# The first norm's vector moved into the first eight units of weights, and the end weighed by VectorE alone

## The chip, the cores and the metric

The kernel runs on one core of a Trainium2 chip. The metric is the device time of one execution in microseconds (us); lower is better. A core has five engines that run beside each other, each through its own instructions in order: TensorE (PE, matrix products, with its weight loads, PEld), VectorE (DVE), ScalarE (ACT), GpSimd (POOL) and SyncE (SP), which here issues the loads. They wait for each other through semaphores.

## The reference

Two layers on x (256 rows of 1024 numbers). A layer is a half-step SwiGLU, a mixing sub-layer of attention and spatial gating, and a second half-step SwiGLU; each has an RMS norm ahead of it and another behind it:

```python
def rms_norm(x, g):
    return x * rsqrt(mean(x * x, axis=-1) + RMS_EPS) * g

def swiglu(x, w1, w2):
    g, u = split(x @ w1, 2, axis=-1)
    return (silu(g) * u) @ w2

for l in range(DEPTH):
    h = rms_norm(x, ffn1_pre_g[l])
    x = x + 0.5 * rms_norm(swiglu(h, ffn1_w1[l], ffn1_w2[l]), ffn1_post_g[l])
    ...                                     # the mixing sub-layer
    h = rms_norm(x, ffn2_pre_g[l])
    x = x + 0.5 * rms_norm(swiglu(h, ffn2_w1[l], ffn2_w2[l]), ffn2_post_g[l])
```

The change is in the first `rms_norm` of the first layer, the product that follows it, and the last `rms_norm`.

## The kernel before

**Numbers as a sum of two.** Each float32 operand of a product is split into a high part, rounded to the format that TensorE reads (a rounding copy on ScalarE), and a low part, the rest (a subtraction on VectorE). A product is three passes into the same PSUM bank: high by high, high by low, low by high (`passes`, L252).

**The stream of weights.** All weights come in units of 128 x 1024 numbers (512 KB) in the order of their use. `Stream.load` issues a unit's load on SyncE into one of four buffers (`raw`, L119). `Stream.upto(n)` splits the units up to number n - 1: ScalarE's copy (L138), VectorE's subtraction (L152), and then the load that may reuse the buffer, four units on. A product calls for its unit by itself if the program has not split it before. The order of the instructions on every engine is the order in which the program's lines run (a manual schedule): what stands later in the program stands later in each engine's queue.

**The start.** The 256 rows are two tiles, t = 0 and 1; a tile has two halves of 512 features, h = 0 and 1 (four blocks of 128 features each). The program loads x in halves, between the first units. TensorE warms up on the identity (`warm`, L972), and transposes x's halves (L217). `weigh` (L943) multiplies them by the norm's vector g0, and `high0` (L947) and `low0` (L950) split them. The first eight units, 0 to 7, are the first 512 columns of w1's gate half (units 0 to 3) and of its other half (units 4 to 7). They are multiplied by rows that are weighed but not yet divided by their root mean square; `finish` scales the result (L314, L315). Unit u needs the blocks 2 (u mod 4) and the next one of both tiles: 12 multiplications of 128x512. Units 0, 1, 4 and 5 use the half h = 0, the others h = 1. `some`, `part` and `units` only write out the order.

**The hand-over.** Meanwhile ScalarE sums the squares of x (L177), VectorE makes the two reciprocal roots (`rsqrt`, L185 to L200) and puts them on two diagonals (L232), and TensorE spreads them over all partitions (`spread`, L239), from which ScalarE copies `rb` (L241). VectorE multiplies each quarter (tile t, half h) by it (L1023), and the quarter is split into `xt` (L947 and L950 again). From unit 8 on, `feature_pair` (L272) multiplies by `xt`: its first four instructions need the quarters with h = 0, the fifth those with h = 1. Before, the program calls for units 5, 6 and 7 ahead of unit 4's products, for unit 8 after the two quarters of tile 0, and for unit 9 after those of tile 1.

**The end.** `project` without a next sub-layer (L467 to L511) adds the last product's norm to x. For tile 1, ScalarE sums squares (L177) and takes a root (L488), VectorE refines its reciprocal in two rounds (L500, L505), and the second half of the product is weighed by the norm's vector in two pieces: VectorE takes 128 columns (L502) and GpSimd 384 (L495), from a copy that ScalarE makes (L494), since GpSimd can't read PSUM here. Then VectorE adds both halves (L444) and they are stored.

Of the kernel before, what the change touches and what calls it, by code (L numbers as in the profile page):

```python
# [14 lines left out]
F32R = mybir.dt.float32r  # L15
# [5 lines left out]
P = 128  # L21
D = 1024
# [29 lines left out]
TURN = 1  # L52
TURN1 = 1

CUT = 128

WARM = (11, 8)

ATTEND = (27, 32, 38, 44, 50, 56)
GATING = (9, 10, 11, 12)  # L60
# [3 lines left out]
def trunk(ctx: ExitStack, tc: tile.TileContext, a: dict, out: bass.AP):  # L64
# [35 lines left out]
    class Stream:  # L100
        def __init__(self):
            self.src, self.where = [], []
            self.raw, self.split = {}, {}
            self.loaded = self.ready = 0
            self.free = RING
            self.rest = None
            self.slip = False

        def add(self, src, where="ring"):
            self.src.append(src)  # L110
            self.where.append(where)
            return len(self.src) - 1

        def load(self, n):

            while self.loaded < min(n, len(self.src)):
                u = self.loaded
                self.raw[u] = new(rawp, [P, 1024], "raw")
                nc.sync.dma_start(self.raw[u], self.src[u])  # L119
                self.loaded += 1  # L120

        def upto(self, n, spare=0):


            while self.ready < min(n, len(self.src)):
                u = self.ready
                if self.where[u] == "ring":
                    if self.free <= spare:
                        return
                    self.free -= 1  # L130
                self.load(u + 1)
                if self.where[u] == "ring":
                    h, lo = new(ring, [P, 1024], "wh", F32R), new(ring, [P, 1024], "wl", F32R)
                else:
# [3 lines left out]
                nc.scalar.copy(h, self.raw[u])  # L138
                self.split[u] = (h, lo)
                self.ready += 1  # L140
                self.low()
                self.rest = u
                if not self.slip:
                    self.low()

        def low(self):

            if self.rest is not None:
                u = self.rest
                self.rest = None  # L150
                h, lo = self.split[u]
                nc.vector.tensor_tensor(out=lo, in0=self.raw.pop(u), in1=f(h), op=ALU.subtract)  # L152
                self.load(u + 1 + RAW)

        def __getitem__(self, u):
# [16 lines left out]
    def halves():  # L172
        return [slice(h * 512, (h + 1) * 512) for h in range(2)]
# [229 lines left out]
    def project(units, lhs, k_post, gpost, gpre, nxt, xt, behind=None):  # L403
# [63 lines left out]
        if nxt is None:  # L467

            root = new(tiny, [P, 1], "rb")
            nc.scalar.activation(root, ones[:, 0:1], AF.Sqrt)  # L470
            head(0)
            c = new(t2, [P, 512], "t2")
            nc.scalar.copy(c, o[0][1])
            nc.gpsimd.tensor_tensor(out=og[0][:, 512:D], in0=c, in1=gpost[:, 512:D], op=ALU.mult)
            r, = rsqrt([(total(parts[0]), k_post)])
            for h, b in enumerate(halves()):
                add(0, h, r)
                nc.sync.dma_start(out[rows_of(0), b], xs[0][:, b])

            head(1)  # L480
            k = 0.25 ** k_post
            vb = new(tiny, [P, 1], "rv")
            nc.vector.tensor_scalar(out=vb, in0=parts[1][:, 0:1], scalar1=D * RMS_EPS, scalar2=k, op0=ALU.add,
                                    op1=ALU.mult)
# [3 lines left out]
            nc.scalar.activation(root, parts[1][:, 1:2], AF.Sqrt, bias=vb, scale=k)  # L488
            w = new(tiny, [P, 1], "rw")
            nc.vector.scalar_tensor_tensor(out=w, in0=parts[1][:, 1:2], scalar=-0.5 * k, in1=vw, op0=ALU.mult,  # L490
                                           op1=ALU.add)
            c0, c1, c2 = 512, 512 + CUT, D
            c = new(t2, [P, 512 - CUT], "t2")
            nc.scalar.copy(c, o[1][1][:, CUT:])  # L494
            nc.gpsimd.tensor_tensor(out=og[1][:, c1:c2], in0=c, in1=gpost[:, c1:c2], op=ALU.mult)  # L495
            r = new(tiny, [P, 1], "ry")
            nc.vector.reciprocal(r, root)
            for i in range(2):
                v = new(tiny, [P, 1], "rt")
                nc.vector.scalar_tensor_tensor(out=v, in0=r, scalar=w, in1=r, op0=ALU.mult, op1=ALU.mult)  # L500
# [4 lines left out]
                nc.vector.scalar_tensor_tensor(out=y, in0=v, scalar=1.5, in1=r, op0=ALU.add, op1=ALU.mult)  # L505
# [405 lines left out]
    for b in halves():  # L911
        nc.sync.dma_start(xs[0][:, b], a["x"][0:P, b])
    st.load(1)
    for b in halves():
        nc.sync.dma_start(xs[1][:, b], a["x"][P:2 * P, b])
# [22 lines left out]
    def quarter0(t, h):  # L938
        return slice(None), slice(h * 4, h * 4 + 4), rows_of(t)

    def weigh(t, h, ps):
        ks = slice(h * 4, h * 4 + 4)
        nc.vector.tensor_tensor(out=xg[t][:, ks, :], in0=ps, in1=g0[:, ks].unsqueeze(2).to_broadcast([P, 4, P]),  # L943
                                op=ALU.mult)

    def high0(x, t, h):
        nc.scalar.copy(x[0][quarter0(t, h)], xg[t][:, h * 4:h * 4 + 4, :])  # L947

    def low0(x, t, h):
        nc.vector.tensor_tensor(out=x[1][quarter0(t, h)], in0=xg[t][:, h * 4:h * 4 + 4, :],  # L950
                                in1=f(x[0][quarter0(t, h)]), op=ALU.subtract)

    one = []
    for t in range(NT):
        first.begin(t)
        one.append(first.steps(t, *xu)[3])

    def units(u, tiles=range(NT)):

        for t in tiles:  # L960
            for k in range(2):
                one[t](u // 4, u % 4 * 2 + k)

    def part(u, t, which):

        for k in range(2):
            one[t](u // 4, u % 4 * 2 + k, which)

    def warm(n):

# [2 lines left out]

    cold = bank()
    warm(WARM[0])
    ps = [transpose4(xs[0], h * 4) for h in range(2)]
    weigh(0, 0, ps[0])
    weigh(0, 1, ps[1])
    high0(xu, 0, 0)
    low0(xu, 0, 0)  # L980
    st.upto(1)
    high0(xu, 0, 1)
    low0(xu, 0, 1)
    warm(WARM[1])
    part(0, 0, (0, 2))
    ps = [transpose4(xs[1], h * 4) for h in range(2)]
    part(0, 0, (1,))
    weigh(1, 0, ps[0])
    st.upto(2)
    high0(xu, 1, 0)  # L990
    low0(xu, 1, 0)
    weigh(1, 1, ps[1])
    part(1, 0, (0, 2))
    part(0, 1, (0, 1))
    part(1, 0, (1,))
    st.upto(3)
    high0(xu, 1, 1)
    low0(xu, 1, 1)
    part(0, 1, (2,))
    part(2, 0, (0, 2))  # L1000
    part(1, 1, (0, 1, 2))
    st.upto(5)
    part(2, 0, (1,))
    part(2, 1, (0, 1, 2))
    sums = []
    for t in range(NT):
        parts = new(tiny2, [P, 2], "parts")
        for h, b in enumerate(halves()):
            square(parts, h, xs[t][:, b])
        sums.append(parts)  # L1010
    r01 = rsqrt([(total(parts), 5) for parts in sums])
    dg = diagonal(r01)
# [7 lines left out]
    for t in range(NT):  # L1020
        for h in range(2):
            ks = slice(h * 4, h * 4 + 4)
            nc.vector.tensor_tensor(out=xg[t][:, ks, :], in0=xg[t][:, ks, :], in1=bc4(rb[:, t, :]), op=ALU.mult)  # L1023
            high0(xt, t, h)
            low0(xt, t, h)
        st.upto(9 + t)
        units(5 + t)
    units(7)
    st.upto(8 + AHEAD)
    subs[0].prepare()  # L1030
# [79 lines left out]
```

## Time and profile before

| what | value |
|---|---|
| median of 3 runs | 1188.09 us (1187.77 to 1188.12) |
| the profiled execution | 1190.44 us, its span 1188.7 us |
| TensorE busy | 1173.2 us, 99% of the span |
| VectorE, ScalarE, GpSimd busy | 836.3, 678.4, 60.0 us |
| read from HBM | 218.65 MB, 185 GB/s over the span |
| TensorE's first multiplication by weights, and its run without gaps | from 7.86, from 10.81 us |
| last multiplication | starts at 1180.93 us |

The span goes from the first to the last instruction of the program; the profiled execution's time has 1.74 us around it. A row of a timeline has the start, the duration, the engine, the line, the operation, what it writes and reads (names without buffer numbers, shapes), and how many instructions are merged; in brackets stands the idle time of the engine before it and what ended it. A row of the groups has the line, engine, operation, shapes and count, then busy us and mean ns of one, then idle time. A row of the chain of waits has start, duration and what the end of the kernel was waiting for at that time.

### The profile page before, as it was taken

How to read it: one execution, taken by the hardware profiler on the slowest of the kernel's cores; microseconds unless marked ns; L12 is line 12 of the kernel's file. 1: busy time of each engine (PE TensorE's matmuls, PEld its weight loads, DVE VectorE, ACT ScalarE, POOL GpSimd, SP SyncE). 2: the span in 40 equal slices, each digit the busy share in tenths (PEclk: the TensorE clock that was granted, in tenths of full speed). 3: DMA queues.
4: the chain of work that ended last, by engine and by line, in shares of the span. 5: the costliest groups of instructions: out<-in, count | busy, mean ns of one | idle time of the engine just before them, and what ended most of it. 6: DMA issues, size and time to landing. Idle time of an engine off the chain costs nothing.

```text
span 1188.7 us, 18407 instructions
## 1 busy us (share of the span) xinstructions
PE 1173.2 (99%) x7031; PEld 1044.6 (88%) x7031; DVE 836.3 (70%) x1423; ACT 678.4 (57%) x1143; POOL 60.0 (5%) x40
## 2 busy tenths in 40 slices
PE   8999999998999999999999999999999999999997
PEld 7888888998999888888888888889999998888886
DVE  6768748778685976666586666578878668676753
ACT  5656644547676555664455665455577664665541
POOL 0000000001112100000000000000011040000000
PEclk9999999999999999999999999999999999999999
DMA  7577673554456636657725767645644653565660
GB/s 248 179 247 227 229 245 134 193 196 142 127 154 202 210 107 213 207 183 263 227 95 179 235 202 238 216 154 178 201 139 140 192 193 129 178 199 198 197 204 36
DMA packets 61288, 220.90 MB, mean 186 GB/s; under 512 B 7056, under 2 KB 7056, under 8 KB 61200
## 3 DMA queue, kind: packets, MB, share of 16 engines
q1 hardware_dynamic: 60912, 219.46, 56.8%
q8 instruction: 55, 0.90, 0.3%
q14 instruction: 33, 0.27, 0.1%
q10 hardware_dynamic: 288, 0.27, 0.1%
HBM read 218.65 MB, written 1.05 MB: 185 GB/s over the span
## 4 chain that ended last, share of the span: by engine, by line
PE 92%; DVE 3%; DMA 3%; ACT 1%; issue 1%; SPq 0%; DVEq 0%; ACTq 0%
PE mm L272 34%; PE mm L252 33%; PE mm L259 7%; PE mm L260 7%; PE mm L261 7%; DMA raw<-in_w_in 2%; PE mm L217 1%; PE mm L756 1%; DVE wl L152 1%; PE mm L720 1%; PE mm L719 1%; DMA raw<-in_ffn_w 1%; PE mm L769 0%; PE mm L768 0%; ACT wh L138 0%
## 5 line engine op out<-in xcount | busy, mean ns | idle before, releaser
L152 DVE TENSOR_TENSOR wl<-raw,wh 128x1024 fp32r<-128x1024 f32 x372 | 455.6, 1250 | 117.5 <-ACT wh L138 116.1
L138 ACT CAST wh<-raw 128x1024 fp32r<-128x1024 f32 x372 | 383.0, 1050 | 177.3 <-DMA raw<-in_ffn_w 70.4
L272 PE MATMUL mm<-xt,wh 128*128 128x512 f32 x1152 | 290.7, 393 | 0.7 <-DVE xt L950 0.7
L252 PE MATMUL mm<-wh,m 128*128 128x512 f32 x832 | 258.4, 390 | 0.0
L272 PEld LDWEIGHTS mm<-xt,wh 128*128 128x128 f32 x1152 | 207.3, 189 | 38.6 <-DVE xt L950 1.2
L252 PEld LDWEIGHTS mm<-wh,m 128*128 128x128 f32 x832 | 156.2, 188 | 32.1
L272 PEld LDWEIGHTS mm<-xt,wl 128*128 128x128 f32 x1152 | 157.1, 190 | 11.3
L252 PE MATMUL mm<-wl,m 128*128 128x512 f32 x416 | 161.9, 389 | 0.0
L272 PE MATMUL mm<-xt,wl 128*128 128x256 f32 x1152 | 160.6, 282 | 0.0
L259 PE MATMUL mm<-xt,wh 128*128 128x256 f32 x512 | 146.8, 287 | 0.0
L261 PE MATMUL mm<-xt,wl 128*128 128x256 f32 x512 | 145.3, 284 | 0.0
L260 PE MATMUL mm<-xt,wh 128*128 128x256 f32 x512 | 145.3, 284 | 0.0
L634 DVE TENSOR_TENSOR t<-mm,t 128x256 f32<-128x256 f32 x144 | 60.6, 421 | 97.0 <-ACT t L633 97.0
L260 PEld LDWEIGHTS mm<-xt,wh 128*128 128x128 f32 x512 | 98.8, 193 | 0.2
L259 PEld LDWEIGHTS mm<-xt,wh 128*128 128x128 f32 x512 | 98.8, 193 | 0.2
L261 PEld LDWEIGHTS mm<-xt,wl 128*128 128x128 f32 x512 | 98.6, 193 | 0.0
L252 PEld LDWEIGHTS mm<-wl,m 128*128 128x128 f32 x416 | 78.1, 188 | 16.0
L633 ACT COPY t<-mm 128x256 f32<-128x256 f32 x144 | 52.9, 368 | 46.6 <-PE mm L272 46.5
L259 PE MATMUL mm<-m,wh 128*128 128x256 f32 x256 | 72.5, 283 | 0.0
L260 PE MATMUL mm<-m,wh 128*128 128x256 f32 x256 | 72.4, 283 | 0.0
L261 PE MATMUL mm<-m,wl 128*128 128x256 f32 x256 | 72.4, 283 | 0.0
L636 ACT ACTIVATE t<-t 128x256 f32<-128x256 f32 x72 | 30.1, 418 | 73.8 <-DVE t L634 73.8
(156 smaller groups left out, 1324.3 us busy)
## 6 DMA issues: line engine op xcount, KB each, us to landing
raw<-in_ffn_w SPq DMA_DIRECT2D x264, 512.0 KB, 4.5
raw<-in_w_in SPq DMA_DIRECT2D x84, 512.0 KB, 4.3
raw<-in_w_sgu_branch SPq DMA_DIRECT2D x16, 512.0 KB, 3.7
raw<-in_w_attn_branch SPq DMA_DIRECT2D x16, 512.0 KB, 4.3
raw<-in_w_out SPq DMA_DIRECT2D x16, 512.0 KB, 4.6
gain<-in_ffn_post_g SPq DMA_DIRECT2D x4, 512.0 KB, 6.5
gain<-in_ffn_pre_g SPq DMA_DIRECT2D x3, 512.0 KB, 7.4
x<-in_x SPq DMA_DIRECT2D x4, 256.0 KB, 4.3
```

The lines of the kernel that those rows point to most:

```text
L138: nc.scalar.copy(h, self.raw[u])
L152: nc.vector.tensor_tensor(out=lo, in0=self.raw.pop(u), in1=f(h), op=ALU.subtract)
L217: nc.tensor.transpose(ps[:, k, :], src[:, (c0 + k) * P:(c0 + k + 1) * P], ident)
L252: nc.tensor.matmul(o, every[i][0], every[i][1], start=start and i == 0, stop=stop and i == 2)
L259: nc.tensor.matmul(o, wh[:, ks], ah[:, k, :], start=(k == 0), stop=False)
L260: nc.tensor.matmul(o, wh[:, ks], al[:, k, :], start=False, stop=False)
L261: nc.tensor.matmul(o, wl[:, ks], ah[:, k, :], start=False, stop=(k == KD - 1))
L272: nc.tensor.matmul(out_, w[:, k * P:(k + 1) * P], x, start=(i == 0), stop=(i == len(todo) - 1))
L633: nc.scalar.copy(y[:, half, :], o[half][:, S:2 * S])
L634: nc.vector.tensor_tensor(out=y[:, half, :], in0=o[half][:, 0:S], in1=y[:, half, :], op=ALU.add)
L636: nc.scalar.activation(y[:, 0, :], y[:, 0, :], AF.Silu)
L719: nc.tensor.matmul(s[r][:, i, :], q_, kth[:, g, 0:nk], start=True, stop=False)
```

## The change

Four things. The first transfers are ordered anew: x's half (0, 0), unit 0 in two halves, x's half (1, 0), unit 1, x's halves (0, 1) and (1, 1), units 2 and 3. The norm's vector g0 is taken out of the rows and put into units 0 to 7 while these are split: each half of a unit (one block of features) is rounded by an activation with a scale (`high`), and its low part is one multiply-and-subtract (`lower`). x's transposed rows are split straight from PSUM, without `weigh`; they stay in their banks until they are normalized, so `norm` multiplies them by g0 and by `rb` in four instructions of 128x128 for each quarter, and one bank is emptied by a copy ahead of the spread. And the order of the lines is a new one: units 3 to 7 are now called for one by one, each just ahead of its products, units 5, 6 and 7 behind `spread`, `norm(0, 0)` and `norm(1, 0)`, and unit 8 behind all the quarters. At the end, `weigh_o(1, 1)`, a VectorE instruction of 128x512, replaces the copy, GpSimd's part and VectorE's 128 columns. The warm-up between the first transposes and the first product has five instructions instead of eight.

```diff
-CUT = 128
-
-WARM = (11, 8)
+WARM = (11, 5)
...
-        def load(self, n):
+        def load(self, n, parts=1):
...
-                nc.sync.dma_start(self.raw[u], self.src[u])
+                for i in range(parts):
+                    b = slice(i * 1024 // parts, (i + 1) * 1024 // parts)
+                    nc.sync.dma_start(self.raw[u][:, b], self.src[u][:, b])
...
+        def first(self):
...
+            for i in range(2):
+                self.high(0, (i,))
+                yield
+                self.lower(0, (i,))
+                yield
+            del self.raw[0]
+            self.load(1 + RAW)
+
+        def high(self, u, which=(0, 1)):
+            h = self.split[u][0]
+            if u not in self.gain:
+                nc.scalar.copy(h, self.raw[u])
+                return
+            for i in which:
+                b = halves()[i]
+                nc.scalar.activation(h[:, b], self.raw[u][:, b], AF.Copy, scale=self.gain[u][i])
+
+        def lower(self, u, which=(0, 1)):
+            h, lo = self.split[u]
+            if u not in self.gain:
+                nc.vector.tensor_tensor(out=lo, in0=self.raw[u], in1=f(h), op=ALU.subtract)
+                return
+            for i in which:
+                b = halves()[i]
+                nc.vector.scalar_tensor_tensor(out=lo[:, b], in0=self.raw[u][:, b], scalar=self.gain[u][i],
+                                               in1=f(h[:, b]), op0=ALU.mult, op1=ALU.subtract)
...
-            c0, c1, c2 = 512, 512 + CUT, D
-            c = new(t2, [P, 512 - CUT], "t2")
-            nc.scalar.copy(c, o[1][1][:, CUT:])
-            nc.gpsimd.tensor_tensor(out=og[1][:, c1:c2], in0=c, in1=gpost[:, c1:c2], op=ALU.mult)
+            weigh_o(1, 1)
...
-                if i == 0:
-                    nc.vector.tensor_tensor(out=og[1][:, c0:c1], in0=o[1][1][:, 0:CUT], in1=gpost[:, c0:c1],
-                                            op=ALU.mult)
...
+    load_x(0, 0)
+    st.load(1, parts=2)
+    load_x(1, 0)
+    st.load(2)
+    load_x(0, 1)
+    load_x(1, 1)
     st.load(RAW)
+
+    for u in subs[0].first.units:
+        st.gain[u] = [g0[:, k:k + 1] for k in (u % 4 * 2, u % 4 * 2 + 1)]
...
+    SOON, LATE = ((0, 0), (0, 2), (1, 0)), ((0, 1), (1, 1), (1, 2))
+
+    def units(u):
+
+        for which in (SOON, LATE):
+            for t in range(NT):
+                some(u, t, which)
...
+    turn0(0, 0)
+    next(begin)
+    high0(xu, 0, 0, turned[0, 0])
+    next(begin)
+    low0(xu, 0, 0, turned[0, 0])
+    next(begin)
+    next(begin)
+    next(begin, None)
     warm(WARM[1])
+    some(0, 0, ((0, 0), (0, 1), (1, 0)))
+    turn0(1, 0)
+    rows0(1, 0)
+    some(0, 0, ((0, 2), (1, 2), (1, 1)))
+    some(0, 1, ((0, 0), (0, 1), (1, 0), (1, 1), (0, 2), (1, 2)))
     st.upto(2)
+    turn0(0, 1)
+    some(1, 0, SOON)
+    turn0(1, 1)
+    rows0(0, 1)
+    rows0(1, 1)
+    some(1, 1, SOON)
+    some(1, 0, LATE)
+    some(1, 1, LATE)
     st.upto(3)
+    units(2)
+    parts = [new(tiny2, [P, 2], "parts") for _ in range(NT)]
+    for h, b in enumerate(halves()):
+        square(parts[0], h, xs[0][:, b])
+    st.upto(4)
+    for h, b in enumerate(halves()):
+        square(parts[1], h, xs[1][:, b])
+    units(3)
+    r01 = rsqrt([(total(p), 5) for p in parts])
+    dg = diagonal(r01)
     st.upto(5)
-    st.upto(6)
-    units(3)
-    st.upto(8)
+
+    nc.scalar.copy(xg[1][:, 4:8, :], turned[1, 1])
+    turned[1, 1] = xg[1][:, 4:8, :]
     units(4)
     rb = spread(dg)
+    st.upto(6)
...
+    def norm(t, h):
+        for i in range(4):
+            k = h * 4 + i
+            nc.vector.scalar_tensor_tensor(out=xg[t][:, k, :], in0=turned[t, h][:, i, :], scalar=g0[:, k:k + 1],
+                                           in1=rb[:, t, :], op0=ALU.mult, op1=ALU.mult)
+        high0(xt, t, h, xg[t][:, h * 4:h * 4 + 4, :])
+
+    def normed(t, h):
+        low0(xt, t, h, xg[t][:, h * 4:h * 4 + 4, :])
+
+    units(5)
+    norm(0, 0)
+    st.upto(7)
+    norm(0, 1)
+    normed(0, 0)
+    units(6)
+    norm(1, 0)
+    st.upto(8)
+    normed(0, 1)
+    norm(1, 1)
+    normed(1, 0)
+    normed(1, 1)
     units(7)
     st.upto(8 + AHEAD)
```

More of the change, by code (lines that the diff above doesn't have):

```diff
@@ L107, in __init__ @@
             self.slip = False
+            self.gain = {}
         def add(self, src, where="ring"):
@@ L137, in upto @@
                     h, lo = both[:, 0, :], both[:, 1, :]
-                nc.scalar.copy(h, self.raw[u])
                 self.split[u] = (h, lo)
+                self.high(u)
                 self.ready += 1
@@ L150, in low @@
                 self.rest = None
-                h, lo = self.split[u]
-                nc.vector.tensor_tensor(out=lo, in0=self.raw.pop(u), in1=f(h), op=ALU.subtract)
+                self.lower(u)
+                del self.raw[u]
                 self.load(u + 1 + RAW)
@@ L910, in trunk, with load_x @@
     nc.scalar.dma_start(g0, a["gain0"])
[L911 to L915, printed above, removed]
+    def load_x(t, h):
+        nc.sync.dma_start(xs[t][:, halves()[h]], a["x"][rows_of(t), halves()[h]])
+    load_x(0, 0)
[4 more added lines that the diff above has]
+    load_x(1, 1)
     st.load(RAW)
+    for u in subs[0].first.units:
+        st.gain[u] = [g0[:, k:k + 1] for k in (u % 4 * 2, u % 4 * 2 + 1)]
     sinks = new(const, [P, DEPTH, NH], "sinks")
@@ L939, in quarter0, with high0, low0 @@
         return slice(None), slice(h * 4, h * 4 + 4), rows_of(t)
[L941 to L951, printed above, removed]
+    def high0(x, t, h, src):
+        nc.scalar.copy(x[0][quarter0(t, h)], src)
+    def low0(x, t, h, src):
+        nc.vector.tensor_tensor(out=x[1][quarter0(t, h)], in0=src, in1=f(x[0][quarter0(t, h)]), op=ALU.subtract)
     one = []
@@ L956, in trunk, with some @@
         one.append(first.steps(t, *xu)[3])
[L958 to L967, printed above, removed]
+    def some(u, t, which):
+        for k, i in which:
+            one[t](u // 4, u % 4 * 2 + k, (i,))
+    SOON, LATE = ((0, 0), (0, 2), (1, 0)), ((0, 1), (1, 1), (1, 2))
[3 more added lines that the diff above has]
+                some(u, t, which)
     def warm(n):
@@ L975, in trunk @@
     warm(WARM[0])
[L976 to L983, printed above, removed]
-    warm(WARM[1])
[L985 to L988, printed above, removed]
-    st.upto(2)
[L990 to L995, printed above, removed]
@@ L996, in trunk @@
-    st.upto(3)
[L997 to L1001, printed above, removed]
-    st.upto(5)
[L1003 to L1012, printed above, removed]
-    st.upto(6)
-    units(3)
```

20 lines of the change are left out of this document (11 added, 9 removed).

## The prediction

> **What bounds the kernel now.** I read the page first, then the chain of waits up to 45 us, then each engine's timeline there, and last the timeline of the final 10 us.
>
> ```profile
> PE 1173.2 (99%) x7031; PEld 1044.6 (88%) x7031; DVE 836.3 (70%) x1423; ACT 678.4 (57%) x1143; POOL 60.0 (5%) x40
> ```
>
> TensorE is busy for 99% of the span, and the change leaves its multiplications as they are. So it can only move the three places where TensorE isn't fed: the start, the hand-over to the first layer's second group of weights (unit 8 on, L272), and the tail. The chain of waits (start, duration, what) shows the first two:
>
> ```profile
> 3.13 6.55 DMA raw<-in_ffn_w
> 9.71 1.06 ACT m L138
> 10.81 12.53 PE mm L252 x54
> ...
> 23.81 0.38 ACT t L241
> ...
> 33.02 0.70 DVE xt L950
> 33.76 11.26 PE mm L272 x62
> ```
>
> TensorE runs without a gap from 10.81, when unit 1's weights are split: 54 multiplications (12.53 / 54 = 0.23 us each), then the spreading of the norms, whose result ScalarE copies at 23.81 (L241, "rb"). Behind it the chain runs through ScalarE and VectorE, not TensorE, until the last normalized quarter is there at 33.72. The first four multiplications of L272 lie ahead of it:
>
> ```profile
> 31.88 1.17 PE L272 MATMUL mm<-xt,wh 128*128 128x512 f32 x4
> 33.76 0.96 PE L272 MATMUL mm<-xt,wh 128*128 128x512 f32 x3 [0.72 <-DVE xt L950]
> ```
>
> Four are worth 0.91, so the stage that follows starts, in effect, at 33.76 - 0.91 = 32.85, which is 9.04 after rb. From there on TensorE is full, and a shift of this point shifts the end. The stage keeps to 9.04 because units 5, 6 and 7 had been cast before rb, in gaps that cost nobody anything:
>
> ```profile
> 18.14 1.98 ACT L138 CAST wh<-raw 128x1024 fp32r<-128x1024 f32 x2
> 20.89 1.05 ACT L138 CAST wh<-raw 128x1024 fp32r<-128x1024 f32 x1 [0.77 <-DMA raw<-in_ffn_w]
> ```
>
> **Part 1, the start: a gain.** Transfers go in halves and in another order, x's rows are split straight from PSUM, and the first weights are multiplied by the norm's vector (g0) while they are split. What TensorE needs to become continuous is tile 1's first half of x. In the trace (SP's timeline, then the time to landing of the transfers issued at 1.72 and 2.18):
>
> ```profile
> 1.72 0.42 SPq L119 DMA_DIRECT2D raw<-in_ffn_w  x1
> 2.18 0.91 SPq L915 DMA_DIRECT2D x<-in_x  x2
> raw<-in_ffn_w SPq DMA_DIRECT2D x1, 512.0 KB, 5.0
> x<-in_x SPq DMA_DIRECT2D x1, 256.0 KB, 5.5
> ```
>
> With unit 0's weights 1 MB had landed at 1.72 + 5.0 = 6.72; that half of x landed, as the fifth quarter MB, at 2.18 + 5.5 = 7.68. Now it is the fourth quarter: between 6.72 (bytes alone) and 7.68 (nothing gained by the order); I take 7.0, nearer to the bytes, since the queue is one. Four transposes (0.6), the rounding copy (0.62, L947 below) and hand-offs give 8.37 for tile 1's first multiplication; from then on unit 1's and unit 2's weights are early enough. Six of unit 0's multiplications lie before it, as six lie before 10.81 now, so 54 remain in both: 2.44 us earlier. Against that, eight transposes now stand behind this point (8 x 0.11 = 0.87), and unit 4's low part is late: VectorE computes the two reciprocal roots and diagonals just ahead of it,
>
> ```profile
> 18.27 0.16 DVE L207 SCALAR_TENSOR_TENSOR rv<-parts 128x1 f32<-128x1 f32 x1 [0.97 <-ACT t L177]
> 20.55 3.49 DVE L152 TENSOR_TENSOR wl<-raw,wh 128x1024 fp32r<-128x1024 f32 x3
> ```
>
> which is 2.28 us. The squares now stand between the casts of units 2, 3 and 4 and end at about 17.1; with 2.3 and two halves of 0.7 the low part is done at 20.7, where TensorE would want its last half at 20.4. I take 0.45 for this. So rb comes 2.44 - 0.87 - 0.45 = 1.12 earlier, at 22.7 (0.4 to 1.4 earlier, by the two landings).
>
> **Part 2, behind rb: a loss that is larger.** The prices (groups of instructions; the two L314 and L311 differ by a pointer operand):
>
> ```profile
> L314 ACT ACTIVATE t<-mm,ry 128x512 f32<-128x512 f32 x5 | 3.4, 692 | 0.0
> L311 ACT ACTIVATE t<-mm 128x512 f32<-128x512 f32 x3 | 1.8, 602 | 0.0
> L947 ACT CAST n<-t 128x512 fp32r<-128x512 f32 x4 | 2.5, 618 | 3.8 <-DVE t L943 3.8
> L444 DVE SCALAR_TENSOR_TENSOR x<-t,ry,x 128x512 f32<-128x512 f32 x24 | 17.8, 749 | 0.6
> L374 DVE SCALAR_TENSOR_TENSOR vv<-mm,ry,vv 128x128 fp32r<-128x128 f32 x2 | 0.7, 351 | 1.0 <-ACT vv L373 1.0
> 26.92 0.62 ACT L947 CAST xt<-t 128x512 fp32r<-128x512 f32 x1 [1.36 <-DVE t L1023]
> 27.44 1.05 ACT L138 CAST wh<-raw 128x1024 fp32r<-128x1024 f32 x1
> ```
>
> A weighted half of a unit costs ScalarE 0.62 + 0.09 = 0.71. On VectorE it is an instruction like L444, 0.75, a second one 0.66 behind the first (two last 1.41, in the tail's rows below). The normalizing of a quarter, one L1023 of 0.68 now, becomes four like L374: 0.35 each, 0.26 apart by the same overlap of 0.09, together 1.13. A rounding copy (XH) frees ScalarE after 27.44 - 26.92 = 0.52. A low quarter (XL) frees VectorE after 0.60.
>
> What decides is the order. The program now puts the split of unit 5 behind rb, that of unit 6 behind the first normalized quarter, that of unit 7 behind the third, and unit 8 behind the last. ScalarE runs in order: rb waits for TensorE's spread, unit 5's cast is queued behind it, and TensorE waits for that. XH(0,0) waits for VectorE's normalizing, unit 6's cast is queued behind it, and so on; VectorE has the low parts of that unit queued ahead of the next quarter. The work alternates instead of overlapping. From the start of rb:
>
> - rb 0.28, cast of a half 0.71, two low halves 2 x 0.66, quarter 1.13, hand-offs 0.06: 3.49. Unit 5's multiplications start at 1.04.
> - XH 0.52, half of unit 6 0.71, low halves 1.31, quarter (0,1) 1.04, XL 0.60, quarter (1,0) 1.13, hand-offs 0.06: 5.37, so 8.86. Unit 6 starts at 4.77.
> - XH 0.52, half of unit 7 0.71, low halves 1.31, XL 0.60, quarter (1,1) 1.13, hand-offs 0.06: 4.33, so 13.19. Unit 7 starts at 10.14.
> - XH 0.52, cast of unit 8 1.05, hand-off 0.05: L272 starts at 14.81, with all its rows there.
>
> TensorE's 36 multiplications of units 5 to 7 are 8.2 us and lie inside. So the stage grows from 9.04 to 14.81: 5.77 lost, 1.12 won, L272 later by 4.65, at 37.5. Behind it ScalarE and VectorE have 2.8 us for each unit and need 1.2, so the later casts catch up; unit 12's load is issued some 9 us later than now, at about 39, lands by 44 (5.0 as above) and is needed at 48.7.
>
> **Part 3, the tail: a small gain.** Last instructions of VectorE, and GpSimd's one:
>
> ```profile
> 1180.74 0.68 DVE L440 TENSOR_TENSOR t<-mm,gain 128x512 f32<-128x512 f32 x1
> 1181.34 0.14 DVE L483 TENSOR_SCALAR rv<-parts 128x1 f32<-128x1 f32 x1
> 1182.08 0.16 DVE L490 SCALAR_TENSOR_TENSOR rw<-parts,rw 128x1 f32<-128x1 f32 x1 [0.41 <-ACT t L177]
> 1182.41 0.16 DVE L497 RECIPROCAL ry<-rb 128x1 f32<-128x1 f32 x1 [0.17 <-ACT rb L488]
> 1182.61 0.22 DVE L500 SCALAR_TENSOR_TENSOR rt<-ry,rw 128x1 f32<-128x1 f32 x1
> 1182.98 0.84 DVE L505 SCALAR_TENSOR_TENSOR ry<-rt,ry 128x1 f32<-128x1 f32 x1
> 1183.86 0.22 DVE L500 SCALAR_TENSOR_TENSOR rt<-ry,rw 128x1 f32<-128x1 f32 x1
> 1184.12 0.16 DVE L505 SCALAR_TENSOR_TENSOR ry<-rt,ry 128x1 f32<-128x1 f32 x1
> 1184.31 1.41 DVE L444 SCALAR_TENSOR_TENSOR x<-t,ry,x 128x512 f32<-128x512 f32 x2
> 1182.82 0.99 POOL L495 TENSOR_TENSOR t<-t,gain 128x384 f32<-128x384 f32 x1 [4.36 <-ACT t L494]
> ```
>
> Now VectorE weighs all 512 columns behind L490: start 1182.18, free 0.60 later, so the reciprocal moves from 1182.41 to 1182.78. From it to L444 stand 0.20 + 2 x 0.45 = 1.10 (one round is 1184.31 - 1183.86 = 0.45): 1183.88 instead of 1184.31, a gain of 0.43. It exists because the first L505 took 0.84 and the second 0.16: the first ends at 1183.82, just when GpSimd's instruction ends (1183.81), and GpSimd has nothing to do there any more. The Trainium skill (SBUF — State Buffer, Who interferes with whom) says that a VectorE instruction with two inputs in SBUF is blocked for the whole of a GpSimd instruction that reads SBUF. By that rule the sum is -0.43. If the 0.84 had another cause and stayed, it would be +0.25, and the total 4.9 instead of 4.2.
>
> **The sum.** 4.65 - 0.43 = +4.2. The profiled execution took 1190.44 (span 1188.7, and 1.74 around it) and lies 2.35 above the median, 1188.09; against it I forecast 1194.6, and for the median 1192.3.
>
> **The rivals.** First, the same order with cheaper parts: pointer operands that cost nothing (halves 0.62 and 0.69, small ones 0.29) shorten the stage by about 1.6 and bring rb 0.4 forward, so the sum is +2.2, 1190.3; an early landing takes off another 0.4. Against it stand the rows of L314 and L311. Chance 0.15.
>
> Second, on the other side: the splits of units 5 to 7 overlap the normalizing after all (if the engines' queues don't hold what the program's order says). Then VectorE's sum is the bound: low halves 3 x 1.31, quarters 4 x 1.04, XL 4 x 0.60, 10.5 us in all, of which only unit 5's 1.3 can go ahead of rb. That leaves 9.2, as now, and 1.1 + 0.4 are won: 1186.6, within 0.2%. Only if TensorE itself were the bound (8.2 behind rb, L272 at 30.6) would it be 2.2 + 0.4, 1185.4. For it speaks that ScalarE idles most of the stage; against it, that the trace shows every engine in the program's order. Chance 0.09, a third of it for the faster end.
>
> Third, the clock. The first rows of TensorE:
>
> ```profile
> 1.42 2.61 PE L972 MATMUL mm<-ident 128*128 128x128 f32 x11 [1.42 <-POOL ident masks.py:199]
> 4.87 1.04 PE L972 MATMUL mm<-ident 128*128 128x128 f32 x8
> 7.86 0.96 PE L252 MATMUL mm<-m,n 128*128 128x512 f32 x3 [1.95 <-ACT m L138]
> ```
>
> At the start a transpose takes 0.21, later 0.11; the change of pace comes after 2.7 us of work. My longest new gap is that ahead of unit 7, 10.14 - 4.77 - 2.7 = 2.6 us, then 2 us ahead of L272. If the clock fell in one, a restart at half pace for 2.7 us would cost 1.4: 1193.7. Now the gap of 1.95 ahead of the third row leaves the pace as it was. The Trainium skill (TensorE: Matmul & The Clock Gate, What's actually happening) lets the clock fall after an idle window of about 3.4 us; no gap here is so long, and by that rule the cost is nothing. Chance 0.08.
>
> **How the numbers follow.** About 2.4 us, 0.2%, is what a measurement of this kernel can tell from no change. Forecast 0.68 (slower), cheaper parts 0.15 (0.13 within 0.2%, 0.02 slower), overlap 0.09 (0.06 within, 0.03 faster), clock 0.08 (slower). Faster 0.03, within 0.2% 0.19, slower 0.78. The range reaches down to cheaper parts with an early landing, 1189.8, and up to the clock's case with a late landing, 1194.6.
>
> **What would show it.** Right, if in the new profile rb stands at about 22.7, if the waits of TensorE for casts of units 5, 6 and 7 (L138's successors) are about 1, 1 and 2.5 us, if L272 starts at about 37.5, and if the second L505 of the tail looks like the first. Wrong, if a cast of unit 6 or 7 runs ahead of the normalized quarter that stands before it in the program, if halves cost what half of L138 costs, or if L272 starts before 35.

## The result, and the profile after

| | before | after |
|---|---|---|
| median, same chip | 1187.81 us (1185.82 to 1188.12, 6 runs) | 1194.81 us (6 runs, five of them from 1192.2 to 1196.76) |
| the profiled execution | 1190.44 us, span 1188.7 | 1195.0 us, span 1193.1 |

The ratio is 1.0063 (95% interval 1.0048 to 1.0078): 7.5 us slower. The sixth run of the changed kernel, at 1446 us, had a granted clock of 0.75 where the others had 0.995 to 0.998, and the ratio leaves it out; without it the median is 1194.62. "Slower" was forecast, with 4.2 us; 1194.81 lies 0.2 above the range.

The page after, first line of the busy times. TensorE has 3.9 us more busy time for three instructions fewer, so some of its work ran more slowly; the rest of the loss is waiting.

```profile
PE 1177.1 (99%) x7028; PEld 1044.7 (88%) x7028; DVE 837.7 (70%) x1439; ACT 681.8 (57%) x1151; POOL 59.1 (5%) x39
```

TensorE's timeline after, at the start and in the hand-over (L285 is the old L252, L305 the old L272, L250 the old L217, L143 the activation that casts a weighted half):

```profile
7.01 1.12 PE L285 MATMUL mm<-m,n 128*128 128x512 f32 x3 [1.36 <-ACT n L977]
8.31 0.88 PE L250 MATMUL mm<-ident,x 128*128 128x128 f32 x4 [0.18 <-DMA x<-in_x]
8.84 3.79 PE L285 MATMUL mm<-m,n 128*128 128x512 f32 x9
...
26.47 1.81 PE L285 MATMUL mm<-wh,n 128*128 128x512 f32 x6 [1.08 <-ACT wh L143]
...
30.23 1.81 PE L285 MATMUL mm<-wh,n 128*128 128x512 f32 x6 [0.58 <-ACT wh L143]
...
35.63 2.71 PE L285 MATMUL mm<-wh,n 128*128 128x512 f32 x6 [2.22 <-ACT wh L143]
...
40.40 0.96 PE L305 MATMUL mm<-xt,wh 128*128 128x512 f32 x3 [0.15 <-ACT wh L139]
```

Two things stand in these rows. The waits of 1.08, 0.58 and 2.22 us, each ended by a cast of units 5, 6 and 7, are the alternation that was forecast. And nine multiplications in 3.79 us (0.42 each, where the prediction's 54 took 0.23) are at half pace: TensorE's granted clock was 0.50 there and 1.00 before and after (the windows are in the last section). ScalarE's timeline has rb and the first unit behind it:

```profile
4.47 1.28 ACT L143 ACT_TABLE_LOAD   x1 [4.47 <-DMA raw<-in_ffn_w]
...
25.42 0.37 ACT L274 COPY t<-mm 128x256 f32<-128x256 f32 x1 [3.96 <-PE mm L272]
25.69 1.34 ACT L143 ACTIVATE wh<-raw,g 128x512 fp32r<-128x512 f32 x2
```

rb, the start of the copy from the spread, forecast at 22.7, stands at 25.42. From rb to L305 it is 40.40 - 25.42 = 14.98; 14.81 was forecast. The tail, VectorE's timeline: both small rounds are alike now.

```profile
1187.90 0.16 DVE L532 SCALAR_TENSOR_TENSOR ry<-rt,ry 128x1 f32<-128x1 f32 x1
1188.10 0.22 DVE L530 SCALAR_TENSOR_TENSOR rt<-ry,rw 128x1 f32<-128x1 f32 x1
1188.35 0.16 DVE L532 SCALAR_TENSOR_TENSOR ry<-rt,ry 128x1 f32<-128x1 f32 x1
1188.55 1.42 DVE L477 SCALAR_TENSOR_TENSOR x<-t,ry,x 128x512 f32<-128x512 f32 x2
```

So the large term and the small one came out, and the start did not. The experiments ask three things: is it the order of the splits that costs (1, 4); what made rb late (2, 3, 5, 6, 10); and is the tail's gain GpSimd's (7, 9). Two more look for a better version (8, 11). Kernels 1 to 4, 5 to 8 and 9 to 11 shared a chip and its runs of the kernel before: medians 1186.69, 1186.35 and 1186.01 us.

### The profile page after: what moved, and what is told of

Its sections match the earlier page's. It is cut to its first block, busy times and chain, and to the rows that moved or that the text cites. A ratio compares the mean times of both kernels' runs of the same rounds, so it can differ in the third digit from the quotient of the medians.

```text
span 1193.1 us, 18423 instructions
## 1 busy us (share of the span) xinstructions
PE 1177.1 (99%) x7028; PEld 1044.7 (88%) x7028; DVE 837.7 (70%) x1439; ACT 681.8 (57%) x1151; POOL 59.1 (5%) x39
## 3 DMA queue, kind: packets, MB, share of 16 engines
HBM read 218.65 MB, written 1.05 MB: 184 GB/s over the span
## 4 chain that ended last, share of the span: by engine, by line
PE 86%; DVE 5%; DMA 4%; ACT 2%; issue 1%; SPq 0%; DVEq 0%; ACTq 0%
PE mm L305 33%; PE mm L285 31%; PE mm L292 6%; PE mm L293 6%; PE mm L294 6%; DMA raw<-in_w_in 2%; DVE wl L148 2%; DMA raw<-in_ffn_w 1%; PE mm L250 1%; PE mm L783 1%; ACT wh L139 1%; PE mm L747 1%; PE mm L746 1%; DMA x<-in_x 1%; DVE wl L152 0%
## 5 line engine op out<-in xcount | busy, mean ns | idle before, releaser
L305 PE MATMUL mm<-xt,wh 128*128 128x512 f32 x1152 | 290.6, 393 | 0.6 <-ACT t L347 0.5
L285 PE MATMUL mm<-wh,m 128*128 128x512 f32 x832 | 258.5, 390 | 0.0
L305 PEld LDWEIGHTS mm<-xt,wh 128*128 128x128 f32 x1152 | 207.4, 189 | 38.3 <-ACT t L347 0.8
L285 PEld LDWEIGHTS mm<-wh,m 128*128 128x128 f32 x832 | 156.2, 188 | 32.2
L305 PEld LDWEIGHTS mm<-xt,wl 128*128 128x128 f32 x1152 | 157.2, 190 | 11.3
L285 PE MATMUL mm<-wl,m 128*128 128x512 f32 x416 | 161.9, 389 | 0.0
L305 PE MATMUL mm<-xt,wl 128*128 128x256 f32 x1152 | 160.6, 282 | 0.0
L285 PEld LDWEIGHTS mm<-wl,m 128*128 128x128 f32 x416 | 78.1, 188 | 15.9
```

The lines of the kernel that those rows point to most:

```text
L285: nc.tensor.matmul(o, every[i][0], every[i][1], start=start and i == 0, stop=stop and i == 2)
L305: nc.tensor.matmul(out_, w[:, k * P:(k + 1) * P], x, start=(i == 0), stop=(i == len(todo) - 1))
```

## The experiments

**1. The splits of units 5, 6 and 7 ahead of the spread**, in the kernel after.

```diff
-    st.upto(5)
+    st.upto(8)
...
     rb = spread(dg)
-    st.upto(6)
...
     norm(0, 0)
-    st.upto(7)
...
     norm(1, 0)
-    st.upto(8)
```

> The changed kernel, with one line moved: units 5, 6 and 7 are split ahead of unit 4's products and of the spread, as in the kernel before. Theory (the order: these splits stand behind rb and behind the normalized quarters in ScalarE's and VectorE's queues): rb stays at 25.4 us, but L305 starts about 9 us behind it and not 15, near 34.5; the time falls by about 5.9 at that point, to within 2 us of the kernel before. Rival (the loss comes from dearer instructions or from the clock of TensorE): L305 stays behind 39, the time falls by less than 1.5 us.

1186.51 us (1185.34 to 1191.51), ratio to the kernel before 0.9997 (0.9978 to 1.0016). VectorE, ScalarE and TensorE:

```profile
25.36 2.15 DVE L1064 SCALAR_TENSOR_TENSOR t<-mm,g,t 128x128 f32<-128x128 f32 x8
```
```profile
23.92 0.37 ACT L274 COPY t<-mm 128x256 f32<-128x256 f32 x1 [0.81 <-PE mm L272]
```
```profile
32.50 1.67 PE L305 MATMUL mm<-xt,wh 128*128 128x512 f32 x6 [0.41 <-ACT wh L139]
```

Eight of the normalizing instructions now follow one another without a split between them, and L305 stands 8.58 behind rb instead of 14.98, 6.40 less. rb itself stands 0.5 further behind the second transposes (7.70 to 23.92, 16.22 us, where experiments 2, 3 and 10 have 15.7): the copy that empties a bank for the spread (L1054, at 22.55) is queued behind the casts now. So some 5.9 of the loss is the order, and it takes nearly all of the change's time back. That rb is 1.5 earlier than in the kernel after comes from TensorE's full pace in this execution (1.4) and from transposes 0.6 earlier, less that 0.5.

**2. ScalarE's table loaded first**, in the kernel after: a tiny activation ahead of everything.

```diff
     nc.gpsimd.memset(ones, 1.0)
+    nc.scalar.copy(new(tiny, [P, 1], "early"), ones[:, 0:1])
```

> The changed kernel, with one more ScalarE instruction at the start, a copy of one column of ones, so that the activation table is loaded at 1.3 us and not behind the wait for unit 0's first half (4.47 to 5.75 us). Theory (tile 1's half of x, which lands at 8.28, is what the start waits for): the first multiplication by weights comes 1.28 us earlier, at 5.7, but rb stays within 0.4 us of 25.4. Rival (the table sets the start): rb comes 1.2 us earlier.

1192.51 us. The table load moved from 4.47 to 1.24 and TensorE's first product from 7.01 to 5.59, but then TensorE waits for x:

```profile
8.04 0.66 PE L250 MATMUL mm<-ident,x 128*128 128x128 f32 x4 [1.27 <-DMA x<-in_x]
...
38.75 1.45 PE L305 MATMUL mm<-xt,wh 128*128 128x512 f32 x5 [1.58 <-ACT wh L139]
```

rb stands at 23.79, 1.6 earlier than in the kernel after. The theory had it unmoved and the rival 1.2 earlier, yet it wasn't the table, since the 1.4 us that it set free became a wait; the half pace is missing here (from the transposes to rb it is 15.75, as in experiment 10 without an early table). From rb to L305 it is 14.96 again.

**3. TensorE kept busy at the start**, in the kernel after: 20 warm-up instructions between the first transposes and the first product.

```diff
-WARM = (11, 5)
+WARM = (11, 20)
```

> The changed kernel, with 20 warm-up transposes instead of 5 between the first transposes and the first product, so that TensorE is busy from 3.8 to about 7.2 us. Theory (TensorE fell to half pace at 8.6 us for 3.4 us because it had idled before, and its eight multiplications then cost 0.2 us more each): no half pace between 8 and 12 us, the transposes of x's second halves come 1.7 us earlier, and rb with them, at 23.7. Rival (ScalarE's queue sets rb whatever TensorE does at 9 to 12 us): rb stays within 0.4 us of 25.4. A third possibility: the half pace comes by a window that the warm-ups don't move, and all stays.

1194.5 us (1192.25 to 1196.81, 4 runs), ratio 1.0066 (1.0045 to 1.0087). In the profiled execution (1192.84) there is no half pace, rb is at 24.08 and L305 at 39.04. Experiments 2 and 10 have no half pace either, with five warm-up instructions, so this execution doesn't show that twenty prevent it. The median is that of the kernel after: two of the four executions took over 1196 us, and nothing here says why.

**4. The late order alone**, in the kernel before.

```diff
-    st.upto(6)
     units(3)
-    st.upto(8)
     units(4)
     rb = spread(dg)
+    st.upto(6)
...
     units(5)
     norm(0, 0)
+    st.upto(7)
...
     norm(1, 0)
+    st.upto(8)
```

> The kernel before, with the changed kernel's order alone at the hand-over: units 5, 6 and 7 split behind rb, behind the first and the third normalized quarter, unit 8 behind the last; weights not weighted, quarters normalized by one instruction each. Theory (the order costs the time): from the start of rb to L272's continuous run it takes 13.7 us instead of 9.0, so 4.6 us later there; over the whole, 2 to 5 us slower than the kernel before, since the attention stage has a wait of 2.7 us that a later TensorE would lose. Rival (the dearer weighted halves are what costs): less than 1.5 us later at L272.

1191.24 us (1190.66 to 1192.99), ratio 1.0041 (1.0026 to 1.0056). TensorE:

```profile
37.36 1.89 PE L272 MATMUL mm<-xt,wh 128*128 128x512 f32 x7
```

rb is at 23.79 as before, and L272 starts 13.57 behind it: 37.36 - 32.85 = 4.5 later, for nothing but the order. The change's own stage is 1.4 longer than this one, by the dearer halves and quarters.

**5. The kernel before, once more.**

> The kernel before, unchanged, profiled once more. Its first profile has a wait of 2.66 us in the attention stage (L719 for L846, at 269.9 us) and TensorE at half pace for 3.4 us right behind it, which cost 4.2 us together; the profiles of the changed kernel and of the first experiments have neither. Theory (both belong to that one execution and not to the kernel): they are missing here, and the execution takes about 1186 us, not 1190.4. Rival (the kernel before always has the wait, and a later start only uses it up): the wait is there again, over 2 us.

1187.07 us, where its first profiled execution took 1190.44. That one held a wait of 2.66 us at 272.57 (L719) and half pace behind it, both missing here. Its comparison with the kernel after, span with span (1193.1 - 1188.7 = 4.4), shows too small a loss for that reason. But this execution has something of its own. TensorE:

```profile
8.64 2.08 PE L252 MATMUL mm<-m,n 128*128 128x512 f32 x4 [2.20 <-ACT m L138]
10.52 1.80 PE L217 MATMUL mm<-ident,x 128*128 128x128 f32 x8
...
35.49 0.96 PE L272 MATMUL mm<-xt,wh 128*128 128x512 f32 x3 [0.74 <-DVE xt L950]
```

Eight transposes took 1.04 in the first profile and take 1.80 here: the kernel before has the half pace at the start too, in some executions. rb is then at 25.53 and L272's fifth multiplication 1.73 later than the prediction's 33.76; a part of this can be unit 0's weights, which landed 0.8 later than in the first profile (5.8 us after their issue instead of 5.0).

**6. x ahead of unit 0's weights**, in the kernel after, with the table loaded first.

```diff
-    st.load(1, parts=2)
     load_x(1, 0)
+    st.load(1, parts=2)
```

> The changed kernel with the early table load of the second experiment, and with tile 1's first half of x loaded ahead of unit 0's halves. Theory (rb stands 15.7 us behind the landing of that half, as it did with and without the early table load): the half lands before 5.5 us, the queue of casts moves up until unit 0's weights limit it, and rb comes 0.7 to 1.5 us earlier than with the early table alone (23.8), at 22.3 to 23.1. Rival (ScalarE's own queue, squares among the casts, sets rb): rb stays within 0.4 us of 23.8.

1193.74 us. ScalarE, TensorE, and the landing of the transfer issued at 1.25:

```profile
5.63 0.72 ACT L143 ACTIVATE m<-raw,g 128x512 fp32r<-128x512 f32 x1 [2.90 <-DMA raw<-in_ffn_w]
...
24.95 0.37 ACT L274 COPY t<-mm 128x256 f32<-128x256 f32 x1 [3.96 <-PE mm L272]
```
```profile
6.87 1.42 PE L285 MATMUL mm<-m,n 128*128 128x512 f32 x3 [1.67 <-ACT n L978]
8.09 1.06 PE L250 MATMUL mm<-ident,x 128*128 128x128 f32 x4
```
```profile
x<-in_x SPq DMA_DIRECT2D x1, 256.0 KB, 3.3
```

x has landed at 4.55, 2.7 to 3.7 us sooner than with the other order, and its transposes still start at 8.09: now three multiplications stand ahead of them, which wait for ScalarE's casts of unit 0 and of tile 0's rows, and unit 0's weights have moved back. Their first half is cast from 5.63 on, when it has landed, and was from 4.34 on in experiment 2. The half pace is in this execution too (four transposes in 1.06 instead of 0.60). From the transposes to rb it is 16.86, and without half pace 15.7 (experiments 2, 3 and 10), which would put rb at 23.8. Neither place in the order brings a gain. (rb itself, 24.95, lies where neither side had it.)

**7. GpSimd's last piece cut from 384 to 128 columns**, in the kernel before (CUT = 384).

> The kernel before, with its last weighing cut otherwise: VectorE takes 384 of the 512 columns and GpSimd 128. Theory (the first L505 takes 0.84 us because VectorE is shut out while GpSimd reads): GpSimd's instruction is shorter and ends ahead of the first L505, which then takes 0.16 us; the tail from the end of L177's last read to the start of L444 falls by 0.4 us or more from 2.26. Rival (the first L505 is slow for another reason): it still takes over 0.6 us.

1186.98 us. VectorE and GpSimd:

```profile
1179.39 0.47 DVE L500 SCALAR_TENSOR_TENSOR rt<-ry,rw 128x1 f32<-128x1 f32 x1
1179.79 0.55 DVE L502 TENSOR_TENSOR t<-mm,gain 128x384 f32<-128x384 f32 x1
1180.25 0.14 DVE L505 SCALAR_TENSOR_TENSOR ry<-rt,ry 128x1 f32<-128x1 f32 x1
```
```profile
1179.39 0.46 POOL L495 TENSOR_TENSOR t<-t,gain 128x128 f32<-128x128 f32 x1 [4.14 <-ACT t L494]
```

The 0.84 us of the first L505 is gone. In its place the first L500, 0.22 elsewhere, takes 0.47 and ends with GpSimd at 1179.86: here and before, the small VectorE instruction that reads only SBUF while GpSimd's runs is held to its end. L502, one of whose inputs is in PSUM, wasn't held in the kernel before: it ran from 1182.77 for 0.29 while GpSimd's ran from 1182.82 to 1183.81. The gain is 0.21 (from the last read of the sums to L444 2.05 instead of 2.26) and not 0.4, because the hold moved and did not vanish, and L502 became longer.

**8. A version meant to be best**: the kernel after with the table and x first, the early splits, and unit 8 split between the quarters as well (`st.upto(9)` behind `norm(1, 0)`).

> The changed kernel with everything that the runs so far favour: units 5 to 7 split ahead of unit 4's products, unit 8 ahead of the last normalized quarter, the table loaded early, tile 1's first half of x ahead of unit 0. Theory: rb at about 23, L305 8.0 to 8.6 us behind it, at 31 to 31.6 (32.85 in effect in the kernel before), the tail 0.47 shorter; 1 to 2 us faster than the kernel before, 0.1 to 0.2%, which five rounds may not tell from no change. Rival (VectorE's work behind rb is the bound, with the dearer halves): L305 no earlier than 32.5, no gain beyond the tail's.

1189.17 us (1187.28 to 1190.05), ratio 1.0021 (1.0012 to 1.0030): slower than the kernel before. VectorE and TensorE (the profiled execution, 1187.28, is the fastest of the eleven):

```profile
31.41 1.22 DVE L148 TENSOR_TENSOR wl<-raw,wh 128x1024 fp32r<-128x1024 f32 x1 [1.64 <-ACT wh L139]
32.55 0.68 DVE L981 TENSOR_TENSOR xt<-t,xt 128x512 fp32r<-128x512 f32 x1
33.15 1.14 DVE L1065 SCALAR_TENSOR_TENSOR t<-t,g,t 128x128 f32<-128x128 f32 x4
```
```profile
35.03 1.86 PE L305 MATMUL mm<-xt,wh 128*128 128x512 f32 x7 [2.35 <-ACT xt L978]
```

This repeats the change's mistake with one unit: VectorE reaches unit 8's low part first, waits 1.64 us for ScalarE's cast, and the last quarter stands behind it.

**9. The tail alone**: the kernel before with `weigh_o(1, 1)` in place of the copy, GpSimd's part and VectorE's 128 columns.

> Part 3 alone: the kernel before, with VectorE weighing the end's 512 columns and GpSimd and the copy left out. Theory (the first L505 was blocked by GpSimd): both small rounds alike, 0.16 us each, and from the last read of the sums to the last additions 1.80 us as in the kernel after, instead of 2.26: 0.46 less, 1186.1 where the kernel before has 1186.5 on the same chip. Rival (the 0.84 us had another cause): one round still takes 0.84, and the time grows by 0.25. The median alone can hardly tell the two apart; the rows can.

1185.97 us (1184.34 to 1187.78), ratio 0.9997 (0.9988 to 1.0006), no difference that the time can show. VectorE:

```profile
1179.95 0.16 DVE L499 SCALAR_TENSOR_TENSOR ry<-rt,ry 128x1 f32<-128x1 f32 x1
1180.14 0.22 DVE L497 SCALAR_TENSOR_TENSOR rt<-ry,rw 128x1 f32<-128x1 f32 x1
1180.39 0.16 DVE L499 SCALAR_TENSOR_TENSOR ry<-rt,ry 128x1 f32<-128x1 f32 x1
1180.59 1.41 DVE L444 SCALAR_TENSOR_TENSOR x<-t,ry,x 128x512 f32<-128x512 f32 x2
```

The last read of the sums ends at 1178.79, so it is 1.80 to L444, as in the kernel after and 0.46 less than before.

**10. The kernel after, once more.**

> The changed kernel once more, unchanged. Theory (the half pace of TensorE at 8.6 to 12.0 us belongs to that execution, not to the program): with x's half again landing at about 8.3 us, rb stands at 25.4 if the half pace is there and at 23.8 to 24.1 if it is not; from rb to L305 14.8 to 15.1 in either case. Rival (the late rb is the program's own): rb at 25.4 without a half pace ahead of it.

1192.14 us. TensorE and ScalarE:

```profile
7.06 1.12 PE L285 MATMUL mm<-m,n 128*128 128x512 f32 x3 [1.10 <-ACT n L977]
8.02 0.60 PE L250 MATMUL mm<-ident,x 128*128 128x128 f32 x4
8.38 2.58 PE L285 MATMUL mm<-m,n 128*128 128x512 f32 x9
...
38.69 1.88 PE L305 MATMUL mm<-xt,wh 128*128 128x512 f32 x7 [1.58 <-ACT wh L139]
...
50.50 1.89 PE L305 MATMUL mm<-xt,wh 128*128 128x512 f32 x7 [0.36 <-ACT t L347]
```
```profile
23.73 0.37 ACT L274 COPY t<-mm 128x256 f32<-128x256 f32 x1 [3.97 <-PE mm L272]
```

The nine multiplications take 2.58 instead of 3.79, rb is at 23.73, and from there to L305 it is 14.96. So 1.7 of the late rb belonged to the first execution: 0.3 to the transposes that started at 8.31 instead of 8.02, and 1.4 to the half pace (from there to rb 17.11 instead of 15.71). The wait of 0.36 at 50.50, for a result of ScalarE in the stage behind, is new against the kernel before. It isn't the late order's alone, since experiments 1, 4 and 11 have waits of 0.37, 0.36 and 0.46 at the same place, two of them with early splits; what brings it was not tested.

**11. Unit 8's cast early, its low part late**, on top of the early splits and the early table load.

```diff
     norm(1, 0)
-    st.upto(8)
+    st.slip = True
+    st.upto(9)
+    st.slip = False
...
     units(7)
+    st.low()
     st.upto(8 + AHEAD)
```

> The splits of units 5, 6 and 7 ahead of the spread, the cast of unit 8 (only the cast, its low part stays behind the quarters) ahead of the last quarter's, and a tiny activation first that loads ScalarE's table. Theory (what cost 2.35 us with unit 8's whole split in that place was VectorE's low part between two quarters): ScalarE has 1.6 us between two quarters and the cast takes 1.05, so no quarter is late, TensorE's own 36 multiplications become the bound, and L305 stands 8.2 us behind rb (8.58 with the cast behind the quarters), at 32.0 to 32.3. The time is 0.4 less than with the early splits alone: 1186.1 to 1186.4, within the measurement of the kernel before. Rival (a cast between two quarters is as bad as a low part): L305 10 us behind rb, at 34.

1186.6 us (1185.16 to 1188.15), ratio 1.0003 (0.9994 to 1.0012). ScalarE and TensorE:

```profile
29.79 1.05 ACT L139 CAST wh<-raw 128x1024 fp32r<-128x1024 f32 x1
30.97 0.62 ACT L978 CAST xt<-t 128x512 fp32r<-128x512 f32 x1
```
```profile
32.02 1.75 PE L305 MATMUL mm<-xt,wh 128*128 128x512 f32 x7
```

A cast fits between two quarters where a whole split did not, and TensorE runs from unit 5 into L305 without a gap, 8.01 behind rb. The step was as expected, and the time does not show it: L305 is 0.83 earlier than the 32.85 of the kernel before, but 0.46 of this goes at 43.81, in the wait for ScalarE's result that experiment 10 has too. No version here beats the kernel before by more than a measurement tells.

## Why the prediction was wrong

**Part 2, the hand-over: right.** 14.81 was forecast, 14.96 to 14.98 were measured in the five executions with this order, the kernel after and experiments 2, 3, 6 and 10. The order makes it: experiment 4 adds 4.5 us to the kernel before by the order alone, and experiment 1 takes some 5.9 off the kernel after. The prices held: two halves take 1.34 on ScalarE and two low halves 1.41 on VectorE, a quarter 1.12. The waits came in their places, about 1, 1 and 2.5 forecast, 1.08, 0.58 and 2.22 measured.

**Part 3, the tail: right.** 0.43 was forecast, 0.46 measured in the rows (experiment 9; the time of the kernel can't show so little). By the Trainium skill (SBUF — State Buffer, Who interferes with whom) a VectorE instruction with two inputs in SBUF contends with a GpSimd instruction that reads SBUF, for ports that are locked to one of the two. The trace agrees, with 0.47 for an instruction of 0.22 that ends with GpSimd's (experiment 7).

**Part 1, the start: this step failed.** "So rb comes 2.44 - 0.87 - 0.45 = 1.12 earlier, at 22.7." Like with like, nothing is won: without half pace rb is at 23.81, 23.79 and 23.98 with the old start (the first profile and experiments 4 and 7) and at 23.73 and 23.79 with the new one (10 and 2); with half pace it is at 25.53 and 25.64 with the old one (5 and 9) and at 25.42 with the new one. The working behind the transposes was right: 22.7 - 7.0 = 15.7 was forecast from there to rb, and 23.73 - 8.02 = 15.71 was measured. What failed is the 7.0 itself, the landing of x as the one thing that the transposes wait for: they begin between 7.70 and 8.33 in all eight executions with the new start.

First, x lands later than 7.0. Issued fourth, at 2.18, it took 6.1 us in the first execution of the kernel after, and 5.1 in the second:

```profile
x<-in_x SPq DMA_DIRECT2D x1, 256.0 KB, 6.1
```
```profile
x<-in_x SPq DMA_DIRECT2D x1, 256.0 KB, 5.1
```

Over the six executions with this order of transfers it lands at 7.3 to 8.3, and as the fifth quarter MB, over the five with the old order, at 7.7 to 8.3. The prediction's 6.72 and 7.68 came from one execution, the earliest of these five.

Second, the transposes stand in TensorE's order behind three multiplications that need ScalarE's casts of unit 0 and of tile 0's rows, and these casts stand behind a table load of 1.28 us which ScalarE begins only when the weights have landed (at 4.47). In the kernel before the same load is over long before ScalarE's first cast, at 5.36, so the change itself put it on the path:

```profile
1.24 1.28 ACT L947 ACT_TABLE_LOAD   x1 [1.24 <-PEq L1103]
```

Where one of the two was taken away, the other limit was as late: with the table first x was late (8.04), with x first and the table first unit 0 was (8.09). I had counted one arrival where there were two, both between 7 and just over 8; the table load's place wasn't in the working at all. Transposes ahead of the three multiplications, with x and the table first, were not tried.

**The clock: underrated.** It had a chance of 0.08, for a restart at half pace behind the long waits of the hand-over. It came there, ahead of unit 7's multiplications, and cost nothing, since ScalarE and VectorE set the pace in that stage (14.98 from rb to L305, where executions without it have 14.96). But it also came at the start, where TensorE does set the pace, and cost 1.4 us (experiment 10). Four of the 13 profiled executions have it at the start, two of them with the old start (experiments 5 and 9).

**The sum.** Like with like: 0 at the start, +5.84 in the hand-over (38.69 - 32.85), +0.36 at 50.50, -0.46 in the tail: +5.7 us. Of the 1.5 between this and the forecast 4.2, 1.12 is the start's gain that did not come, and 0.36 is the wait at 50.50, which had no term. Single executions of the kernel after without half pace at the start lie 6.1 and 5.8 above the medians of before (experiments 10 and 2). The 7.5 of the ratio holds in addition executions of 1195 to 1197 us; of one of them, the profiled one, 1.7 of the 2.9 above experiment 10 are the start's, and 1.1 arise later in the execution. That 1.1, and the two executions of over 1196 us in experiment 3, stay open. Three small sums of the prediction don't close, without weight for the argument: by its own terms the upper end is 1193.7 + 0.7 = 1194.4, the lower one 1190.3 - 0.4 = 1189.9, and TensorE as the bound puts L272 at 22.7 + 8.2 = 30.9.

## What to carry to other kernels

Where two engines in order take turns on one chain, don't put work between its links that another engine has to begin: put it ahead of the chain while they idle, or, if it must stand there, only the part whose engine has the room (a cast of 1.05 in a gap of 1.6, and not the low part with it). For an instruction that is to start sooner, list everything that stands ahead of it on its own engine and what each of those waits for: moving one arrival gains nothing if a second one comes at the same time. And profile both kernels more than once before reading differences of 2 us.

## What the runs showed of the hardware

TensorE's clock doesn't follow the length of a gap. The granted clock changes only at the ends of windows of 3.41 us that run through an execution from a phase of its own: in the first execution of the kernel after it rises at 5.19, falls at 8.60, rises at 12.01, falls at 35.91, which are 1, 1 and 7 such windows apart. Here are windows of several executions (bounds, length, TensorE's busy time and its instructions, then the other engines' and the granted clock, behind POOL's, the DMA share and GB/s). The kernel after, first execution:

```profile
5.19:8.60 3.41, 1.87 (x10) 1.07 (x9) 2.01 (x3) 2.38 (x4) 0.00 (x0) 1.00 0.91 302
8.60:12.01 3.41, 3.41 (x12) 2.70 (x11) 2.04 (x3) 1.82 (x3) 0.00 (x0) 0.50 1.04 423
32.50:35.91 3.41, 1.19 (x6) 0.69 (x5) 2.10 (x7) 2.20 (x4) 0.00 (x0) 1.00 0.49 154
```

The kernel after, second execution (experiment 10), with the same gap of 2.2 us ahead of unit 7 and no fall:

```profile
29.89:33.31 3.42, 1.84 (x8) 1.16 (x7) 2.72 (x10) 1.29 (x3) 0.00 (x0) 1.00 0.55 153
33.31:36.72 3.41, 2.78 (x11) 2.10 (x12) 2.80 (x7) 1.19 (x2) 0.00 (x0) 1.00 0.23 22
```

The kernel before, first execution (no fall), and again (experiment 5, a fall at 8.67):

```profile
4.16:7.57 3.41, 1.74 (x16) 1.50 (x14) 1.98 (x3) 1.43 (x2) 0.00 (x0) 1.00 0.95 294
```
```profile
5.26:8.67 3.41, 1.21 (x12) 0.97 (x10) 1.78 (x4) 1.74 (x3) 0.00 (x0) 1.00 0.95 359
```

The same gap lies across two windows in one execution and empties one in another. Over all 13 traces, without the last windows, in which TensorE's work ends, each window with less than 1.4 us of TensorE work was followed by half pace (six of them), none with more than 1.9 was, and of nine with 1.7 to 1.9 two were. So between 1.7 and 1.9 the busy time alone doesn't settle it. This is read off the traces and was not tested by a run of its own. The Trainium skill (TensorE: Matmul & The Clock Gate, What's actually happening) states a free-running window of 3413 ns, and the traces agree; it lets the clock fall after an idle window, and the traces differ: a window filled to a third, 1.19 of 3.41, is enough. With that rule I had asked whether a gap is as long as a window, where the question was how much of a window it may empty.
